# Attention on one Trainium2 core: the second exponential stays in PSUM, row sums come from rounded parts and a ones column, and groups end in fp32 products

## The chip, the cores and the metric

The kernel runs on one core of a Trainium2 chip. The metric is the time of one execution on the device in microseconds (us). The engines are TensorE (PE in the profile, with its weight loads as PEld), VectorE (DVE), ScalarE (ACT), GpSimd (POOL) and SyncE (SP), which issues transfers. Each takes its instructions in the order in which they were put down; they wait for one another by semaphores.

## What is computed

One layer of a streaming encoder, for 2048 prompt tokens and 64 sample tokens: an input projection, attention with eight heads beside a depthwise convolution, an output projection, a feed-forward block and a gated embedding. The change lies in attention. Cut to that:

```python
def attend_chunk_causal(q, k, v):            # prompt: 2048 queries, 2048 keys
    mask = k_chunk[None, :] <= q_chunk[:, None]       # chunks of 64
    sc = jnp.einsum('bqhd,bkhd->bhqk', q_blk, k).astype(jnp.float32) * scale
    pr = jax.nn.softmax(jnp.where(mask, sc, NEG), axis=-1).astype(v.dtype)
    return jnp.einsum('bhqk,bkhd->bqhd', pr, v)

def attend_open(q, k, v):                    # sample: 64 queries, 256 cached keys and 64 new ones
    sc = jnp.einsum('bqhd,bkhd->bhqk', q, k).astype(jnp.float32) * (QK_DIM ** -0.5)
    pr = jax.nn.softmax(sc, axis=-1).astype(v.dtype)
    return jnp.einsum('bhqk,bkhd->bqhd', pr, v).reshape(b, s, ATTN_W)
```

A query and a key have 96 channels, a value has 64. All is fp32.

## The kernel before

The kernel has three phases: input projection with the convolution beside it, attention (`phase2`), and the rest of the layer. To keep fp32 accuracy from a reduced product type (fp32r), a number is held as a rounded part and a rest, `hi` and `lo`; `mm3` (lines 179 to 181) makes a product as hi x hi + lo x hi + hi x lo.

Attention goes over eight heads and, in each, over five groups: four of 512 prompt queries (with 4, 8, 12 and 16 key tiles of 128) and one of the 64 sample queries (three key tiles). Per head and group there are two streams of steps. `maxima` loads the queries, makes one product of the rounded operands per 512 keys into a `tr` bank (line 714) and takes the row maxima from it on VectorE (line 715); the negated maxima go into a spare row of the queries. `attend` then goes over the key tiles. For each it makes the transposed scores (keys on partitions, up to 512 queries as columns; on the diagonal 512, 384, 256 and 128) into an `mm` bank of PSUM. ScalarE reads that bank twice: `ph` is the exponential rounded to fp32r (line 752), `px` the same exponential in fp32 (line 753), both in SBUF. VectorE makes `pl = px - ph` (line 754). GpSimd adds all `px` of the group into the first one (line 758), for the row sums. TensorE multiplies `v`, which holds the 64 hi and 64 lo columns of the values side by side, by `ph` (line 761) and by `pl` (line 762), both into the bank `acc`.

At the end of a group ScalarE copies `acc` to `ot` (line 765). TensorE transposes each token tile of `ot` (line 769), ScalarE copies one half (line 772) and VectorE adds the other (line 773). TensorE also transposes the sums (line 775), VectorE reduces them over keys to `su` (line 777) and takes reciprocals (line 779).

What sets the order: the two streams are interleaved by their columns, `maxima` running ahead by `AHEAD`; then a scheduler with a model of the chip orders the instructions of each engine. `banks` gives out the eight PSUM banks: in attention `mm` goes round two of them, then three, `tr` round four, and `acc` has one. `PXB` and `PHB` are the numbers of SBUF buffers of `px` and of `ph` and `pl`.

Of the kernel before, what the change touches and what calls it, by code (L numbers as in the profile page):

```python
# [9 lines left out]
F32 = mybir.dt.float32  # L10
# [38 lines left out]
PXB = 7  # L49
PHB = 5  # L50
# [17 lines left out]
class Body:  # L68
    def __init__(self, nc, tc, ctx, I, O):
# [10 lines left out]
        # reciprocal softmax sums of every token and head  # L80
        self.ri = self.cp.tile([P, 17, NH], F32, name="ri")

# [21 lines left out]
    def scratch(self):  # L104
# [3 lines left out]
        # scaled queries, channel-major: nope rows of all heads, then first and second halves of their rope rows  # L108
# [3 lines left out]
        # rotated keys, then the rows that meet the masks and maxima  # L112
# [4 lines left out]
    @contextmanager  # L117
    def low(self, off):
        """Instructions traced inside give way to those of the next `off`."""
        self.tc.cur_priority += off  # L120
        yield
        self.tc.cur_priority -= off

    def banks(self, mm, tr, spare):
        """PSUM banks that mm() and tr() go round, and the one of acc()."""
        self.mmi, self.tri, self.spare = cycle(mm), cycle(tr), spare
# [40 lines left out]
    def pin(self, r, n=1):  # L167
        """n steps of the background work, queued behind r on its engine."""
# [14 lines left out]
    def norms(self, xs, tiles, w=D):  # L183
        """Reciprocal root mean squares of the rows of xs (of width w), a column per tile."""
# [9 lines left out]
    def scaled(self, xs, piece, dst):  # L194
        """dst[j] = xs[j] * rstd of its rows (all of width D)."""
# [6 lines left out]
    def operand(self, piece, hs, gc, nk, hi, lo):  # L202
        """hi/lo [128, nk, N] <- transposed hs tiles times gain columns."""
# [18 lines left out]
    def phase1(self):  # L222
        nc, tc, I, O = self.nc, self.tc, self.I, self.O
        self.banks((0, 1, 2, 7), (4, 5, 6), 3)
        with ExitStack() as c:
# [13 lines left out]
            def early_t(piece, hs, i):  # L239
                """Operand of the rows as they are; their norms as columns and, along all partitions, as a row."""  # L240
# [18 lines left out]
            def weights(parts, k, c, eng=None):  # L259
                """Split weights [128, k, c]: per k, (hi, lo) [128, c]."""  # L260
# [14 lines left out]
            def rows(T, w, c, name, width):  # L275
                """Token-major products of a piece with w, to SBUF, and the sums of squares of `width` columns."""
# [20 lines left out]
            def latents(T, w):  # L297
                """c_kv of a piece; its rotated keys to scratch."""
# [20 lines left out]
            def keys(T, kvs):  # L319
                """Split transposed latents of a piece."""  # L320
# [27 lines left out]
            def queries(T, cqs):  # L348
                """Split transposed query latents of a piece; a function that makes the queries."""
# [29 lines left out]
            def glu(T, j, w, n=3):  # L379
                """Channels j of the conv input of a piece, channel-major, to scratch."""  # L380
# [24 lines left out]
            # rows of the norms of block 0, and ones  # L405
# [818 lines left out]
```

## Time and profile before

| | |
|---|---|
| three timed runs, median (lowest to highest) | 3081.51 us (3078.47 to 3082.38) |
| the profiled execution, its span | 3076.4 us |
| TensorE busy | 2940.3 us, 96% of the span |
| VectorE busy | 2047.9 us, 67% |
| ScalarE busy | 1215.2 us, 40% |
| GpSimd busy | 878.3 us, 29% |

The time of the profiled execution is its span and what lies around it. Shares of the whole span mix phases with different limits; attention goes from about 525 to 1110 us. A matmul's end is modelled, so its duration contains a fill that overlaps with the next one: TensorE's pace is read from the distances of starts. Instructions of the other engines overlap their neighbours a little as well.

### The profile page before, as it was taken

The numbers are of one execution on the slowest core, as the hardware profiler recorded it, in microseconds if no ns is written. First come the engines' busy times: TensorE is split into PE (matmuls) and PEld (weight loads), VectorE is DVE, ScalarE is ACT, GpSimd is POOL, SyncE is SP. The second block draws the span as 40 slices with busy tenths as digits, with TensorE's granted clock in tenths as the row PEclk, the third lists the DMA queues.
The fourth block names the chain that finished last, engine by engine and source line by source line (L and its number), as shares of the span: only waits on it lengthen the run. The fifth ranks groups of instructions, "written<-read, shape, count | busy, mean of one in ns | idle before, by whom it ended". The sixth has DMA issues, their size and how long they took to land.

```text
span 3076.4 us, 42553 instructions
## 1 busy us (share of the span) xinstructions
PE 2940.3 (96%) x15586; PEld 2604.4 (85%) x15586; DVE 2047.9 (67%) x3533; ACT 1215.2 (40%) x2404; POOL 878.3 (29%) x1498
## 2 busy tenths in 40 slices
PE   8998899989989879999999999999999999999998
PEld 7997888667667769999999888998998799999986
DVE  4489693999999866666665556787775544444453
ACT  6443342767666734222222433222234432321242
POOL 3235555877776730002002020003022100000001
PEclk9999999999998989999999999999999999999999
DMA  6635258743331132111222242232232411221121
GB/s 200 207 115 181 82 167 166 107 66 57 56 53 31 32 123 74 61 57 64 71 84 78 81 162 69 68 108 68 73 109 92 144 48 62 83 76 55 62 92 45
DMA packets 148601, 279.12 MB, mean 91 GB/s; under 512 B 38136, under 2 KB 78824, under 8 KB 146952
## 3 DMA queue, kind: packets, MB, share of 16 engines
q1 hardware_dynamic: 123800, 244.35, 24.7%
q0 software_dynamic: 24592, 32.06, 6.5%
q8 instruction: 122, 2.00, 0.3%
q14 instruction: 87, 0.71, 0.1%
HBM read 225.67 MB, written 51.28 MB: 90 GB/s over the span
## 4 chain that ended last, share of the span: by engine, by line
PE 72%; DVE 15%; DMA 4%; issue 4%; POOL 3%; ACT 1%; SPq 1%; DVEq 0%; POOLq 0%; ACTq 0%
PE mm L179 23%; PE mm L181 23%; PE mm L180 23%; DVE pl L754 6%; DVE mx L715 3%; DVE cacc L614 2%; PE tr L211 2%; PE tr L714 1%; PE acc L762 1%; DMA qr<-q_s 1%; DMA qr<-in_mq 1%; DMA h<-in_x 1%; POOL rt L153 0%; POOL ry L155 0%; DVE su L777 0%
## 5 line engine op out<-in xcount | busy, mean ns | idle before, releaser
L179 PE MATMUL mm<-thi,uh 128*128 128x384 f32 (+2 forms) x1488 | 480.8, 324 | 0.0
L180 PE MATMUL mm<-tlo,uh 128*128 128x384 f32 (+2 forms) x1488 | 480.7, 323 | 0.0
L181 PE MATMUL mm<-thi,ul 128*128 128x384 f32 (+2 forms) x1488 | 480.3, 323 | 0.0
L614 DVE SCALAR_TENSOR_TENSOR cacc<-cu,cw,cacc 128x384 f32<-128x384 f32 (+2 forms) x720 | 445.1, 632 | 7.3
L758 POOL TENSOR_TENSOR px<-px 128x512 f32<-128x512 f32 (+5 forms) x304 | 399.6, 1315 | 124.7 <-ACT px L753 65.4
L179 PE MATMUL mm<-wdh,ah 128*128 128x512 f32 x896 | 349.5, 391 | 4.9 <-DVE x L1060 2.9
L180 PE MATMUL mm<-wdl,ah 128*128 128x512 f32 x896 | 348.8, 390 | 0.0
L181 PE MATMUL mm<-wdh,al 128*128 128x512 f32 x896 | 345.2, 390 | 0.0
L983 ACT ACTIVATE rl<-mm 128x384 f32<-128x384 f32 (+1 forms) x192 | 88.1, 459 | 590.6 <-PE mm L181 590.2
L152 POOL TENSOR_TENSOR rt<-ry 128x3 f32<-128x3 f32 (+2 forms) x150 | 38.0, 254 | 987.0 <-DVE ry L149 980.2
L754 DVE TENSOR_TENSOR pl<-px,ph 128x512 fp32r<-128x512 f32 (+5 forms) x344 | 309.3, 913 | 15.2 <-ACT px L753 14.1
L1060 DVE SCALAR_TENSOR_TENSOR x<-mm,y,x 128x512 f32<-128x512 f32 x224 | 166.6, 749 | 206.9 <-PE mm L181 204.8
L180 PEld LDWEIGHTS mm<-tlo,uh 128*128 128x128 f32 x1488 | 280.2, 188 | 0.5
L179 PEld LDWEIGHTS mm<-thi,uh 128*128 128x128 f32 x1488 | 279.9, 188 | 0.7
L181 PEld LDWEIGHTS mm<-thi,ul 128*128 128x128 f32 x1488 | 280.1, 188 | 0.1
L165 DVE TENSOR_TENSOR wdl<-raw,wdh 128x1024 fp32r<-128x1024 f32 x139 | 170.8, 1230 | 116.7 <-ACT wdh L164 115.5
L752 ACT ACTIVATE ph<-mm 128x512 fp32r<-128x512 f32 (+5 forms) x344 | 179.3, 522 | 119.6 <-PE mm L181 102.4
L164 ACT CAST wdh<-raw 128x1024 fp32r<-128x1024 f32 x139 | 146.0, 1050 | 157.9 <-DMA raw<-in_wdn 87.1
L179 PEld LDWEIGHTS mm<-wdh,ah 128*128 128x128 f32 x896 | 168.3, 188 | 40.6 <-DVE x L1060 3.3
L181 PEld LDWEIGHTS mm<-wdh,al 128*128 128x128 f32 x896 | 168.2, 188 | 35.0
L180 PEld LDWEIGHTS mm<-wdl,ah 128*128 128x128 f32 x896 | 168.3, 188 | 33.7
L602 POOL DMA_DIRECT2D cu<-u_s x20 | 11.2, 558 | 637.9 <-DVE cacc L614 637.5
(297 smaller groups left out, 6854.4 us busy)
## 6 DMA issues: line engine op xcount, KB each, us to landing
raw<-in_wup SPq DMA_DIRECT2D x96, 512.0 KB, 3.2
raw<-in_wdn SPq DMA_DIRECT2D x96, 512.0 KB, 3.2
raw<-in_wglu SPq DMA_DIRECT2D x24, 512.0 KB, 4.6
raw<-in_wout SPq DMA_DIRECT2D x24, 512.0 KB, 4.5
raw<-in_wgate SPq DMA_DIRECT2D x24, 512.0 KB, 3.8
v_s<-vst SPq DMA_DIRECT2D x36, 256.0 KB, 2.8
v<-v_s POOLq DMA_DIRECT2D x8, 1152.0 KB, 9.2
h<-in_x SPq DMA_DIRECT2D x16, 512.0 KB, 4.5
```

The lines of the kernel that those rows point to most:

```text
L164: self.nc.scalar.copy(out=hi, in_=raw)
L165: return (eng or self.nc.vector).tensor_tensor(out=lo, in0=raw, in1=hi.bitcast(F32), op=ALU.subtract)
L179: t.matmul(ps, sh, mh, start=start, stop=False)
L180: t.matmul(ps, sh, ml, start=False, stop=False)
L181: t.matmul(ps, sl, mh, start=False, stop=stop)
L614: nc.vector.scalar_tensor_tensor(out=a, in0=U[:, k:k + W], scalar=w, in1=a, op0=ALU.mult, op1=ALU.add)
L715: nc.vector.tensor_reduce(out=mx[:n, b:b + 1] if nb > 1 else top, in_=ps[:n, :w], axis=AX.X, op=ALU.max, negate=True)
L752: nc.scalar.activation(out=ph[b:, s], in_=ps[:, s], func=AF.Exp)
L754: nc.vector.tensor_tensor(out=pl[b:, s], in0=px[b:, s], in1=ph[b:, s].bitcast(F32), op=ALU.subtract)
L758: nc.gpsimd.tensor_tensor(out=rs[b:, s], in0=rs[b:, s], in1=px[b:, s], op=ALU.add)
L983: nc.scalar.activation(out=rl[:, :N], in_=ps[:, :N], func=AF.Relu)
L1060: r = nc.vector.scalar_tensor_tensor(out=x1[t][:n, cs], in0=ps[:n, :], scalar=Y[q][:n, j:j + 1], in1=x1[t][:n, cs], op0=ALU.mult, op1=ALU.add)
```

## The change

The second exponential is written over the scores, in the same PSUM bank, in place of `px` in SBUF; `pl` reads it there. So the bank is held until `pl` is done. `v` gets two columns of ones, and its hi and lo halves change places: lo, hi, ones. The products with `ph` take all 128 value columns, as before, into `acc`; the products with `pl` take the 64 hi columns and the ones, into a bank of their own, `low`. The product of `pl` with the lo half of the values is no longer made. GpSimd adds up the `ph` in a tile `rs` of its own (a copy for the first key tile); the ones column adds up the `pl`.

A group ends in two copies by ScalarE, `ot` and `ol`, and, per token tile, three fp32 products that add up in one bank: `ol` with 65 columns of the identity, `ot` with `fold` (two identities of 64 stacked: hi plus lo), and `rs` with a column of ones. The result holds the output in 64 columns and the row sum in the 65th. ScalarE copies the output, VectorE takes the reciprocals straight from PSUM. VectorE's `o` and `su` are gone. Banks are now three for `mm`, three for `tr`, one for `acc`, one for `low`, from the start; `PHB` goes from 5 to 6 and `px` is gone.

```diff
-                nc.scalar.copy(out=v[:n, :, 0, :], in_=pv[:n, hs])
-                r = nc.vector.tensor_tensor(out=v[:n, :, 1, :], in0=pv[:n, hs], in1=v[:n, :, 0, :].bitcast(F32),
+                nc.scalar.copy(out=v[:n, :, 1, :], in_=pv[:n, hs])
+                r = nc.vector.tensor_tensor(out=v[:n, :, 0, :], in0=pv[:n, hs], in1=v[:n, :, 1, :].bitcast(F32),
...
-        self.banks((0, 1), (2, 4, 5, 6), 7)
+        self.banks((0, 1, 2), (3, 4, 5), 6)
...
-                V[i] = pool.tile([P, NKT, P], F32R, name=f"v{i}")
+                V[i] = pool.tile([P, NKT, VW], F32R, name=f"v{i}")
+                nc.vector.memset(V[i][:, :, P:].bitcast(F32), 1.0)
...
-                acc = self.acc()
+                acc, low = self.acc(), self.bank(7, "low")
+                rs = p.tile([P, 512], F32, name="rs", bufs=2)
...
-                    nc.scalar.activation(out=ph[b:, s], in_=ps[:, s], func=AF.Exp)
-                    nc.scalar.activation(out=px[b:, s], in_=ps[:, s], func=AF.Exp)
-                    nc.vector.tensor_tensor(out=pl[b:, s], in0=px[b:, s], in1=ph[b:, s].bitcast(F32), op=ALU.subtract)
+                    nc.scalar.activation(out=ph[b:, s], in_=ps[b:, s], func=AF.Exp)
+                    nc.scalar.activation(out=ps[b:, s], in_=ps[b:, s], func=AF.Exp)
+                    nc.vector.tensor_tensor(out=pl[b:, s], in0=ps[b:, s], in1=ph[b:, s].bitcast(F32), op=ALU.subtract)
                     if kt == 0:
-                        rs = px
+                        nc.gpsimd.tensor_copy(out=rs[:, s], in_=ph[:, s].bitcast(F32))
                     else:
-                        nc.gpsimd.tensor_tensor(out=rs[b:, s], in0=rs[b:, s], in1=px[b:, s], op=ALU.add)
+                        nc.gpsimd.tensor_tensor(out=rs[b:, s], in0=rs[b:, s], in1=ph[b:, s].bitcast(F32), op=ALU.add)
...
-                    nc.tensor.matmul(acc[:, s], vk, ph[b:, s], start=kt == 0, stop=False)
-                    nc.tensor.matmul(acc[:, s], vk, pl[b:, s], start=False, stop=last)
+                    nc.tensor.matmul(acc[:, s], vk[:, :P], ph[b:, s], start=first, stop=last)
+                    nc.tensor.matmul(low[:VW - 64, s], vk[:, 64:], pl[b:, s], start=first, stop=last)
...
+                ol = p.tile([P, 512], F32, name="ol", bufs=2)[:VW - 64, :]
+                nc.scalar.copy(out=ol[:, :qn], in_=low[:VW - 64, :qn])
...
-                    nc.tensor.transpose(out=tr[:n, i * P:(i + 1) * P], in_=ot[:, i * P:i * P + n], identity=self.ident)
+                    c, q = 65 * i, slice(i * P, i * P + n)
+                    nc.tensor.matmul(tr[:n, c:c + 65], ol[:, q], self.ident[:VW - 64, :65], start=True, stop=False)
+                    nc.tensor.matmul(tr[:n, c:c + 64], ot[:, q], fold, start=False, stop=False)
+                    nc.tensor.matmul(tr[:n, c + 64:c + 65], rs[:, q], one, start=False, stop=True)
...
-                nc.scalar.copy(out=o[:n, :m, :], in_=x[:, :, 1, :])
-                nc.vector.tensor_tensor(out=o[:n, :m, :], in0=x[:, :, 0, :], in1=o[:n, :m, :], op=ALU.add)
-                for i in range(m):
-                    nc.tensor.transpose(out=sm[:n, i * P:(i + 1) * P], in_=rs[:, i * P:i * P + n], identity=self.ident)
-                su = self.sp.tile([P, 4], F32, name="su")
-                nc.vector.tensor_reduce(out=su[:n, :m], in_=sm[:n, :m * P].rearrange("p (t k) -> p t k", k=P), axis=AX.X,
-                                        op=ALU.add)
-                nc.vector.reciprocal(out=self.ri[:n, tiles[0]:tiles[0] + m, h:h + 1], in_=su[:n, :m].unsqueeze(2))
+                nc.scalar.copy(out=o[:n, :m, :], in_=x[:, :, :64])
+                nc.vector.reciprocal(out=self.ri[:n, tiles[0]:tiles[0] + m, h:h + 1], in_=x[:, :, 64:])
```

The scheduler also puts the instructions in another order. TensorE before, inside the group of 16 key tiles of a head (`k0h` and `k0l` are the keys, `ph_8994` and `pl_8995` came from the scores `mm_8989`, `ph_9011` from `mm_9006`, and the scores `mm_9038` and `mm_9055` lie between these and the two shown):

```order
L179 MATMUL mm_9076<-qh_8314,k0h_5808 128x512
L180 MATMUL mm_9076<-ql_8315,k0h_5808 128x512
L181 MATMUL mm_9076<-qh_8314,k0l_5809 128x512
L714 MATMUL tr_8819<-k0h_5808,qh_8529 128x512
L714 MATMUL tr_8923<-k0h_5808,qh_8913 128x320
L179 MATMUL mm_9092<-qh_8314,k0h_5808 128x512
L180 MATMUL mm_9092<-ql_8315,k0h_5808 128x512
L181 MATMUL mm_9092<-qh_8314,k0l_5809 128x512
L762 MATMUL acc_8926<-pl_8995,v0_5812 128x512
L761 MATMUL acc_8926<-ph_9011,v0_5812 128x512
```

The product with `pl_8995` stands behind five younger score tiles. TensorE now, at the same place (`ph_8982` and `pl_8983` came from the scores `mm_8978`, `pl_8952` from `mm_8947`, `ph_8998` from `mm_8994`):

```order
L179 MATMUL mm_8994<-qh_8272,k0h_5808 128x512
L180 MATMUL mm_8994<-ql_8273,k0h_5808 128x512
L181 MATMUL mm_8994<-qh_8272,k0l_5809 128x512
L762 MATMUL acc_8868<-ph_8982,v0_5812 128x512
L763 MATMUL low_8869<-pl_8952,v0_5812 66x512
L179 MATMUL mm_9014<-qh_8272,k0h_5808 128x512
L180 MATMUL mm_9014<-ql_8273,k0h_5808 128x512
L181 MATMUL mm_9014<-qh_8272,k0l_5809 128x512
L717 MATMUL tr_8908<-k1h_5828,qh_8887 128x128
L717 MATMUL tr_8928<-k1h_5828,qh_8887 128x384
L762 MATMUL acc_8868<-ph_8998,v0_5812 128x512
L763 MATMUL low_8869<-pl_8983,v0_5812 66x512
```

A product with `ph` now follows its scores by one younger tile and one with `pl` by two; over the whole program, the products with `pl` stood behind three to seven younger tiles for most tiles, and stand behind exactly two for 292 of 344.

VectorE before, in the same stretch (`mx` are row maxima, `o` is the output of an earlier group):

```order
L754 TENSOR_TENSOR pl_8995<-px_8993,ph_8994 128x512
L754 TENSOR_TENSOR pl_9012<-px_9010,ph_9011 128x512
L773 TENSOR_TENSOR o_8734<-tr_8728,o_8734 128x256
L715 TENSOR_REDUCE mx_8752<-tr_8785 128x1
L754 TENSOR_TENSOR pl_9044<-px_9042,ph_9043 128x512
```

VectorE now:

```order
L755 TENSOR_TENSOR pl_8952<-mm_8947,ph_8951 128x512
L755 TENSOR_TENSOR pl_8983<-mm_8978,ph_8982 128x512
L718 TENSOR_REDUCE mw0_5818<-tr_8908 128x1
L718 TENSOR_REDUCE mw0_5818<-tr_8928 128x1
L755 TENSOR_TENSOR pl_8999<-mm_8994,ph_8998 128x512
```

The subtraction takes its first operand from the score bank, and the addition of `o` is gone; reductions of maxima stand between subtractions as before.

## Rows read from the trace of the kernel before

**Rows 1.** The head of the page: the span of the profiled execution.

```profile
span 3076.4 us, 42553 instructions
```

**Rows 2.** The timeline of VectorE: start us, duration us, engine, line, operation, count.

```profile
606.75 0.22 DVE L754 TENSOR_TENSOR pl<-px,ph 64x64 fp32r<-64x64 f32 x1
...
1027.12 0.22 DVE L754 TENSOR_TENSOR pl<-px,ph 64x64 fp32r<-64x64 f32 x1
```

**Rows 3.** Busy time of each engine over these six heads, granted clock, DMA.

```profile
606.75:1027.12 420.37, 382.43 (x1777) 296.52 (x1776) 395.15 (x705) 287.58 (x709) 314.82 (x246) 0.94 0.33 54
```

**Rows 4.** Waits in the same stretch: us in total, times, longest us.

```profile
PEld acc L762 <- DVE pl L754: 48.3, 81, 1.2
...
PE acc L762 <- DVE pl L754: 24.4, 52, 0.9
```

**Rows 5.** Groups by line, VectorE, same stretch: count, busy us, mean ns, idle before.

```profile
L754 DVE TENSOR_TENSOR pl<-px,ph 128x512 fp32r<-128x512 f32 (+5 forms) x258 | 230.3, 905 | 11.6 <-ACT px L753 11.4
...
L777 DVE TENSOR_REDUCE su<-tr 128x4 f32<-128x512 f32 (+1 forms) x30 | 17.5, 599 | 5.4 <-PE tr L775 5.2
...
L773 DVE TENSOR_TENSOR o<-tr,o 128x256 f32<-128x256 f32 (+1 forms) x30 | 11.0, 366 | 0.0
```

**Rows 6.** Groups by line and shape in the same stretch, GpSimd and VectorE.

```profile
L758 POOL TENSOR_TENSOR px<-px 128x512 f32<-128x512 f32 x144 | 227.1, 1577 | 73.8 <-ACT px L753 52.0 <-DVE pl L754 12.5
L754 DVE TENSOR_TENSOR pl<-px,ph 128x512 fp32r<-128x512 f32 x168 | 188.1, 1129 | 11.4 <-ACT px L753 11.4
```

**Rows 7.** Lines 773, 1110, 1111 over the whole span: ns shortest/median/longest.

```profile
L773 DVE TENSOR_TENSOR o<-tr,o x40: 183/411/425, 554.6 to 1114.0; 128x256 f32<-128x256 f32 x32, 64x64 f32<-64x64 f32 x8
...
L1110 DVE TENSOR_TENSOR rl<-mm,rl x34: 681/686/692, 1735.6 to 3063.9; 128x512 f32<-128x512 f32 x32, 64x512 f32<-64x512 f32 x2
...
L1111 DVE TENSOR_TENSOR x<-x,rl x34: 679/692/694, 1736.3 to 3064.6; 128x512 f32<-128x512 f32 x32, 64x512 f32<-64x512 f32 x2
```

**Rows 8.** The timeline of GpSimd, four additions in a row.

```profile
669.51 4.58 POOL L758 TENSOR_TENSOR px<-px 128x512 f32<-128x512 f32 x4
```

**Rows 9.** Groups by line, ScalarE, the six heads.

```profile
L753 ACT ACTIVATE px<-mm 128x512 f32<-128x512 f32 (+5 forms) x259 | 134.5, 519 | 0.8 <-POOL px L758 0.8
...
L765 ACT COPY ot<-acc 128x512 f32<-128x512 f32 (+1 forms) x31 | 17.1, 553 | 4.6 <-PE acc L762 4.4
```

**Rows 10.** The timeline of TensorE, 838 to 844 us.

```profile
838.15 0.39 PE L762 MATMUL acc<-pl,v 128*128 128x512 f32 x1
...
841.11 0.53 PE L714 MATMUL tr<-k1h,qh 128*128 128x512 f32 x2
...
843.70 0.34 PE L179 MATMUL mm<-qh,k1h 128*128 128x384 f32 x1
843.88 0.34 PE L180 MATMUL mm<-ql,k1h 128*128 128x384 f32 x1
```

**Rows 11.** The timeline of TensorE in the first phase: transposes, an fp32 product, the next.

```profile
37.09 0.82 PE L211 MATMUL tr<-ident,h 128*128 128x128 f32 x6
37.74 0.81 PE L249 MATMUL tr<-cu,cs 128*128 128x384 f32 x2
38.09 0.63 PE L179 MATMUL mm<-whi,thi 128*128 128x384 f32 x1
38.56 0.33 PE L180 MATMUL mm<-wlo,thi 128*128 128x384 f32 x1
```

**Rows 12.** Busy time in stretches (columns: PE, PEld, DVE, ACT, POOL, granted clock, DMA).

```profile
847.50:850.00 2.50, 1.90 (x9) 1.07 (x8) 2.50 (x4) 1.24 (x4) 2.42 (x2) 1.00 0.00 0
850.00:852.50 2.50, 1.71 (x7) 0.87 (x5) 2.50 (x7) 0.00 (x0) 1.91 (x3) 0.75 0.00 0
...
857.50:860.00 2.50, 2.50 (x7) 1.97 (x6) 0.69 (x1) 2.03 (x4) 0.00 (x0) 0.50 0.00 0
```

More of the change, by code (lines that the diff above doesn't have):

```diff
@@ L48 @@
 AHEAD = 16000
-PXB = 7
-PHB = 5
+PHB = 6
+VW = P + 2
 TILES = [(t * P, P) for t in range(SEQ // P)] + [(SEQ, DEC)]
@@ L675, in load_kv @@
                 v = V[h % 3]
-                nc.gpsimd.dma_start(out=v[:, :NKT - 1, :],
+                nc.gpsimd.dma_start(out=v[:, :NKT - 1, :P],
                                     in_=self.v_s[:(NKT - 1) * P, h, :].rearrange("(t p) d -> p t d", p=P))
-                nc.gpsimd.dma_start(out=v[P - DEC:, NKT - 1, :], in_=self.v_s[(NKT - 1) * P:, h, :])
+                nc.gpsimd.dma_start(out=v[P - DEC:, NKT - 1, :P], in_=self.v_s[(NKT - 1) * P:, h, :])
             def group(g):
@@ L745, in attend @@
                     self.mm3(ps[:, s], kh[:, kk], kl[:, kk], qh[:, s], ql[:, s], True, True)
-                    if kn < P:
-                        ps = ps[P - kn:, :]
-                    px = p.tile([P, 512], F32, name="px", bufs=PXB)
+                    b = P - kn
                     ph = p.tile([P, 512], F32R, name="ph", bufs=PHB)
                     pl = p.tile([P, 512], F32R, name="pl", bufs=PHB)
-                    b = P - kn
-                    nc.scalar.activation(out=ph[b:, s], in_=ps[:, s], func=AF.Exp)
-                    nc.scalar.activation(out=px[b:, s], in_=ps[:, s], func=AF.Exp)
-                    nc.vector.tensor_tensor(out=pl[b:, s], in0=px[b:, s], in1=ph[b:, s].bitcast(F32), op=ALU.subtract)
+                    nc.scalar.activation(out=ph[b:, s], in_=ps[b:, s], func=AF.Exp)
+                    nc.scalar.activation(out=ps[b:, s], in_=ps[b:, s], func=AF.Exp)
+                    nc.vector.tensor_tensor(out=pl[b:, s], in0=ps[b:, s], in1=ph[b:, s].bitcast(F32), op=ALU.subtract)
                     if kt == 0:
-                        rs = px
+                        nc.gpsimd.tensor_copy(out=rs[:, s], in_=ph[:, s].bitcast(F32))
                     else:
-                        nc.gpsimd.tensor_tensor(out=rs[b:, s], in0=rs[b:, s], in1=px[b:, s], op=ALU.add)
+                        nc.gpsimd.tensor_tensor(out=rs[b:, s], in0=rs[b:, s], in1=ph[b:, s].bitcast(F32), op=ALU.add)
                     vk = v[b:, 16 + kt if smp else kt, :]
-                    last = kt == len(kts) - 1
-                    nc.tensor.matmul(acc[:, s], vk, ph[b:, s], start=kt == 0, stop=False)
-                    nc.tensor.matmul(acc[:, s], vk, pl[b:, s], start=False, stop=last)
+                    first, last = kt == 0, kt == len(kts) - 1
+                    nc.tensor.matmul(acc[:, s], vk[:, :P], ph[b:, s], start=first, stop=last)
+                    nc.tensor.matmul(low[:VW - 64, s], vk[:, 64:], pl[b:, s], start=first, stop=last)
                     yield qn - lo * P + 60
@@ L789, in phase2 @@
                 nc.vector.memset(x.bitcast(F32), 0.0)
+            fold = p.tile([P, 64], F32, name="fold")
+            nc.vector.tensor_tensor(out=fold, in0=self.ident[:, :64], in1=self.ident[:, 64:], op=ALU.add)
+            one = p.tile([P, 1], F32, name="one")
+            nc.vector.memset(one, 1.0)
             idr = p.tile([P, P], F32R, name="idr")
@@ L821, in phase2 @@
             ca, cb = -AHEAD, 0
-            for i, c in enumerate(a):
+            for c in a:
                 ca += c
-                if i == 30:
-                    self.banks((0, 1, 2), (3, 4, 5, 6), 7)
                 while cb * wa < ca * wb:
```

4 lines of the change are left out of this document (2 added, 2 removed).

## The prediction, made before the changed kernel was run

> **What bounds the kernel now.** The span is 3076.4 us, in one execution; the three timed runs have a median of 3081.5, 5.1 more, which is what lies around the span [rows 1]. I read the attention by its stretches first, since the change touches nothing else but three small preparations. The smallest score tile of the sample's group comes back once per head: at 606.75 us and, six heads later, at 1027.12, so a head takes 420.37 / 6 = 70.06 us [rows 2]. In that stretch VectorE is busy 395.15 of 420.37 us, 94%, TensorE 382.43 (with the half-speed time in it: mean granted clock 0.94), ScalarE 287.58, GpSimd 314.82 [rows 3]. The waits agree: TensorE's weight loads and matmuls stand 48.3 and 24.4 us for `pl` of VectorE [rows 4]. VectorE sets the pace, and of its time the 258 subtractions `pl` take 230.3 us [rows 5].
>
> Why are they so dear? A 512-wide `pl` takes 1129 ns here, and GpSimd's 512-wide addition 1577 ns [rows 6]. The same VectorE operation, 512 wide with both operands in SBUF, takes 692 ns in the last phase, where GpSimd is nearly idle, and 686 ns with one operand in PSUM. And inside attention, with GpSimd as busy as ever, the one subtract-like operation that has an operand in PSUM and one in SBUF (`o`, 256 wide) stays between 183 and 425 ns over all its 40 calls, median 411 [rows 7]. GpSimd's own addition, when it runs undisturbed, takes 4.58 / 4 = 1.15 us [rows 8]. So two engines reading two SBUF operands each stretch one another, and an operand in PSUM ends that.
>
> **The change part by part**, per head, from the six-head stretch.
>
> *VectorE.* `pl` now reads the second exponential from PSUM. By the 686 ns at 512 and the 411 at 256, a column is 1.07 ns, so 384, 128 and 64 columns take .55, .27 and .21 us. The stretch has 168 tiles of 512, 24 each of 384, 256 and 128, and 18 of 64: 168 x .686 + 24 x (.55 + .41 + .27) + 18 x .21 = 149 us in place of 230. That is 81 us, 13.6 a head. The reduction `su` and the addition `o` go: 17.5 + 11.0 = 28.5, 4.8 a head [rows 5]. VectorE falls from 65.9 to 47.5 us a head, and no longer binds.
>
> *GpSimd.* 38 additions a head become up to .4 us shorter, five copies (at most 1.15 us each) come in: 50 us a head fall to about 43. Off the path.
>
> *ScalarE.* One copy `ol` of the new accumulator more per group, at the price of `ot`: 17.1 us for 31, so 5 x .55 = 2.8 a head. ScalarE goes from 47.9 to 50.7. The second exponential now writes PSUM; no row shows that. Its nearest row is the same exponential into SBUF, 519 ns; I take that, and bound it by .1 us either way, 43 tiles, 4 us a head. ScalarE would still end below TensorE [rows 9].
>
> *TensorE.* Thirteen 512-column products start from 838.15 on until the next one at 841.11: (841.11 - 838.15) / 13 = .228 us apart, those of 384 columns .18 (I use .174: 128 columns less are .054 less, so 256 take .12), and a short product is held by its weight load: six in a row take .82 us, less the .27 of the last, over 5 = .11 [rows 10, 11]. A head has, for scores and values, 5 products for each of 28 tiles of 512, and for 4 each of 384, 256 and 128, and 3 of 64: 5 x (28 x .228 + 4 x (.174 + .12 + .115) + 3 x .11) = 41.7. The maxima: 28 x .228 + 4 x (.174 + .12 + .115) and some six short ones, 8.7. The group ends: 17 tiles x 2 transposes x .12 = 4.1. Sum 54.6 of the 70.06. The change keeps the first two sums (the value products have the same columns) and replaces each pair of transposes by three fp32 products. What does such a product cost? The only fp32 product of the trace that is no transpose, 384 wide, stands as two matmuls: they start at 37.74, and the next product, which lasts .33 when nothing is ahead of it, ends at 38.72, so the pair held TensorE for .65 us [rows 11]. A pass is thus .85 ns a column: 65 columns need .055 us, less than the .11 of a weight load. So a product is two passes of .11, a token tile 6 x .11 = .66 instead of .24, and a head 17 x .42 = 7.1 us more: **61.7 us**. Beneath, if passes overlapped better, 17 x (6 x .055 - .24) = 1.5; above, if a pass cost a full .15, 11. I keep .11, the pace of the nearest row. This is the part of the change that costs.
>
> A rule speaks against this edit: the Trainium skill, "TensorE: Matmul & The Clock Gate", section Terms, says that the transpose mode is 4 times faster for fp32. By columns alone that is 4 x 130 column times for the three products against 256 for two transposes, .12 us a tile at the .445 ns of rows 10, or 2 us a head where I take 7.1; the trace shows the 4 column times in the 384-wide product, but short products are held by their weight loads.
>
> *The clock.* In each head TensorE falls to half speed (1.2 of 2.4 GHz) once: granted clock .75 and then .50 from about 851 to 861 us, after a stretch in which it waited for `pl` [rows 12]. The mean of 0.94 costs 6%, 4 us a head. With `pl` faster that stretch is denser; I count 1.5 us a head left, between 0 and 4.
>
> *The banks.* `mm` now holds a score until `pl` has read it, where a copy in SBUF freed it before. Banks for scores stay three. The order shows it: before, the product with a `pl` follows its own scores by three to seven younger tiles; now by two (292 of 344). From the last score pass, a tile needs .39 for that pass, .50 and .59 for the exponentials, .69 for `pl` and some .1 of signals, 2.3 us, and .46 for the first two passes ahead; three tiles' work on TensorE is 3 x 5 x .228 = 3.4 us without maxima, 4.1 with one each. So a slack of .7 to 1.4 us is there, and one reduction (.60) or copy ahead of the tile uses most of it. The same holds for who is queued behind: ScalarE's exponentials of the next group stand behind `ot` and `ol`, which wait for the group's last products, five times a head. I count 3 us a head of TensorE's waiting, 1.5 to 9; before it was 70.06 - 54.6 - 4 = 11.5.
>
> *At no cost:* the fill of ones, `fold` and `one` (six instructions on VectorE ahead of attention, a few us at most where it has time); the swap of the halves of `v` (same bytes, same rows of 512 bytes); the group end's wait for `rs`, which GpSimd ends within an addition (1.15) of the last exponential, while the value products with `pl` and the copy `ol` take longer. If GpSimd lagged, each of 40 group ends would stall TensorE, since products of other tiles stand behind.
>
> **The sum.** 61.7 + 1.5 + 3 = 66.2 us a head against 70.06: 3.9 x 8 heads = 31 us. 3076.4 - 31 = 3045 of span, **3050.5 us** with the 5.1. So TensorE binds after the change, and most of VectorE's gain (18 us a head) is spent: a part was slack behind TensorE, a part goes into the fp32 products.
>
> **The rivals.**
> 1. *TensorE is filled, clock full.* 61.7 + 0 + 1.5 = 63.2: -6.9 x 8 = -55, **3026**. For it: VectorE now keeps 94% busy, and TensorE would have work queued as well; cheaper fp32 products end here too. Against: three banks and in-order queues.
> 2. *The stretching stays* when the subtraction still reads one operand from SBUF, or GpSimd stretches it otherwise. Then `pl` keeps its 230 us and VectorE has 61.1 a head beside TensorE's 61.7; with 4 of clock and 4 of waits 69.7: **3078**, no change. Against: `o` in rows 7, though it is 256 wide and only 40 calls. The Trainium skill, "SBUF — State Buffer", section Who interferes with whom, says that VectorE contends with GpSimd's reads when both its inputs are in SBUF, and not when one at most is; this lowers the rival's chance, and the rows agree.
> 3. *The banks bind: slower.* If each key tile waits .2 us for its bank, 43 tiles give 8.6 a head, and the clock stays as it is (4): 61.7 + 12.6 = 74.3, +34 us, **3115**. The point from which it decides: waits and clock together above 8.4 us a head. For it: slack of .7 us beside reductions of .6. Against: VectorE and ScalarE are busy only 47.5 and 50.7 of 66.
>
> **How the numbers follow.** Forecast .50, rival 1 .20, rival 2 .12, rival 3 .18. Forecasts and rival 1 end below 3075.3, that is faster by over 0.2% (some 6 us, about what a measurement of this kernel can tell from no change): .70. Rival 2 is the .12 of the same, rival 3 the .18 of slower. The range reaches down to rival 1 less a little, 3022, and up into rival 3 to 3090, which leaves out about a tenth on each side at most.
>
> **What would show it.** In the profile after: `pl` at 512 columns near .69 us and GpSimd's addition near 1.15 (rival 2 if above .9); three fp32 products as six matmuls per token tile, .66 us; VectorE near 70% of attention and TensorE the engine that others wait for; a head near 66 us. Rival 3 shows as score products that wait for `pl` or its bank. Wrong would be a clock that drops oftener, for the short fp32 passes, or ScalarE above 60 us a head, by a dear exponential into PSUM.

## The result, and the profile after

The changed kernel takes 3049.09 us (median of four runs, 3045.0 to 3052.11) against 3081.95 for the kernel before (four runs, 3078.47 to 3085.56): a ratio of 0.9891, with a 95% interval of 0.9877 to 0.9906. The forecast was 3050.5, from 3022 to 3090, and faster. The profiled execution took 3045.0 us, with a span of 3043.2, 33.2 less than before [rows 1].

The head of the page: span, and each engine's busy time, share of the span and instructions; then the shares of the chain that ended last, by engine.

```profile
span 3043.2 us, 43503 instructions
...
PE 2960.0 (97%) x16130; PEld 2636.6 (87%) x16130; DVE 1915.9 (63%) x3458; ACT 1235.8 (41%) x2444; POOL 823.9 (27%) x1538
...
PE 83%; DVE 6%; POOL 4%; DMA 2%; ACT 2%; issue 2%; SPq 0%; ACTq 0%; POOLq 0%; DVEq 0%
```

The timeline of VectorE, with the smallest score tile of the sample's group, as in [rows 2], and under it the busy time of the engines in those six heads (PE, PEld, DVE, ACT, POOL, then granted clock, DMA share, GB/s), as in [rows 3]:

```profile
602.57 0.23 DVE L755 TENSOR_TENSOR pl<-mm,ph 64x64 fp32r<-64x64 f32 x1 [0.20 <-ACT mm L754]
...
998.70 0.23 DVE L755 TENSOR_TENSOR pl<-mm,ph 64x64 fp32r<-64x64 f32 x1 [0.74 <-ACT mm L754]
```

```profile
602.57:998.70 396.13, 392.74 (x2184) 320.49 (x2183) 301.17 (x647) 304.68 (x742) 272.56 (x278) 0.99 0.32 57
```

A head takes 396.13 / 6 = 66.02 us, 4.04 less than the 70.06 of before; eight such heads make 32.3 of the 33.2 us, so little is left for what lies outside attention. TensorE is busy 99% of the stretch, VectorE 76% (94% before).

Groups of instructions in the six heads (count, busy us, mean ns of one, idle before it and what ended that): by line the subtractions; by line and shape, of 512 columns, GpSimd's additions and the subtractions; by line two of ScalarE:

```profile
L755 DVE TENSOR_TENSOR pl<-mm,ph 128x512 fp32r<-128x512 f32 (+5 forms) x259 | 147.0, 575 | 42.8 <-ACT mm L754 40.5
```

```profile
L759 POOL TENSOR_TENSOR rs<-rs,ph 128x512 f32<-128x512 f32 x144 | 185.5, 1288 | 73.2 <-ACT ph L753 66.7
...
L755 DVE TENSOR_TENSOR pl<-mm,ph 128x512 fp32r<-128x512 f32 x168 | 113.9, 683 | 28.5 <-ACT mm L754 26.8
```

```profile
L754 ACT ACTIVATE mm<-mm 128x512 f32<-128x512 f32 (+5 forms) x258 | 131.5, 510 | 0.4
...
L769 ACT COPY ol<-low 66x512 f32<-66x512 f32 (+1 forms) x30 | 15.3, 509 | 0.0
```

The subtraction at 512 columns fell from 1129 to 683 ns and its group from 230.3 to 147.0 us [rows 5, 6]. It now waits 40.5 us for the second exponential, where it waited 11.4 before [rows 5]. TensorE's weight loads stood 48.3 us for `pl` before [rows 4]; these are waits of its weight loads after:

```profile
PEld acc L762 <- ACT ph L753: 9.1, 25, 0.7
PEld mm L179 <- DVE pl L755: 2.5, 3, 1.1
...
PEld low L763 <- DVE pl L755: 1.4, 5, 0.3
```

The last row is the wait that was 48.3 us. The second is the score bank: a score product that waits for the subtraction to free it. It happened three times in six heads. The first, the longest in total, is of products with `ph`, which wait for ScalarE's first exponential.

The timeline of TensorE in a group end, two token tiles:

```profile
777.05 0.44 PE L774 MATMUL tr<-ident,ol 66*128 66x65 f32 x2
777.32 0.39 PE L775 MATMUL tr<-fold,ot 128*128 128x64 f32 x2
777.55 0.33 PE L776 MATMUL tr<-one,rs 128*128 128x1 f32 x2
777.74 0.41 PE L774 MATMUL tr<-ident,ol 66*128 66x65 f32 x2
```

A token tile's products come .67 to .69 us apart, and every product is two matmuls, whether it has 65 columns or one.

### The profile page after: what moved, and what is told of

Its sections match the earlier page's. It is cut to its first block, busy times and chain, and to the rows that moved or that the text cites. A ratio compares the mean times of both kernels' runs of the same rounds, so it can differ in the third digit from the quotient of the medians.

```text
span 3043.2 us, 43503 instructions
## 1 busy us (share of the span) xinstructions
PE 2960.0 (97%) x16130; PEld 2636.6 (87%) x16130; DVE 1915.9 (63%) x3458; ACT 1235.8 (41%) x2444; POOL 823.9 (27%) x1538
## 4 chain that ended last, share of the span: by engine, by line
PE 83%; DVE 6%; POOL 4%; DMA 2%; ACT 2%; issue 2%; SPq 0%; ACTq 0%; POOLq 0%; DVEq 0%
PE mm L179 24%; PE mm L181 24%; PE mm L180 24%; DVE cacc L614 3%; PE acc L762 2%; PE tr L717 2%; PE low L763 2%; PE tr L211 2%; PE tr L774 1%; PE tr L775 1%; ACT ph L753 1%; PE tr L776 1%; POOL rt L153 1%; POOL ry L155 1%; POOL rt L154 0%
## 5 line engine op out<-in xcount | busy, mean ns | idle before, releaser
L759 POOL TENSOR_TENSOR rs<-rs,ph 128x512 f32<-128x512 f32 (+5 forms) x304 | 324.8, 1071 | 106.8 <-ACT ph L753 89.7
L755 DVE TENSOR_TENSOR pl<-mm,ph 128x512 fp32r<-128x512 f32 (+5 forms) x344 | 195.4, 577 | 66.4 <-ACT mm L754 63.7
L718 DVE TENSOR_REDUCE mx<-tr 128x1 f32<-128x512 f32 (+3 forms) x288 | 170.2, 615 | 41.5 <-PE tr L717 40.9
```

The source lines that it names most:

```text
L718: nc.vector.tensor_reduce(out=mx[:n, b:b + 1] if nb > 1 else top, in_=ps[:n, :w], axis=AX.X, op=ALU.max, negate=True)
L755: nc.vector.tensor_tensor(out=pl[b:, s], in0=ps[b:, s], in1=ph[b:, s].bitcast(F32), op=ALU.subtract)
L759: nc.gpsimd.tensor_tensor(out=rs[b:, s], in0=rs[b:, s], in1=ph[b:, s].bitcast(F32), op=ALU.add)
```

## The experiments

"Head" below is a sixth of the stretch between the same small tiles of six heads. "Clock lost" is worked out from the windows of such a stretch, 2.5 us each: the sum of (1 - granted clock) x time. It was 23.9 us in the six heads before, 4.0 a head, and 5.1 after, .85 a head. "Waits" is what is left of a head beside TensorE's own sum (61.7 in the changed kernel, by the forecast) and the clock: 70.06 - 54.6 - 4.0 = 11.5 before, 66.02 - 61.7 - .85 = 3.5 after. So an error in the 61.7 would show as waits. All ratios are to the kernel before, run on the same chip, with the 95% interval in brackets. Differences from the changed kernel go by its 3049.09 us; since the kernel before came to between 3078 and 3082 us from one set of runs to the next, a difference of some 4 us there says little. Figures of a head come from one profiled execution of each kernel.

### Is it the operand in PSUM? The kernel before without the additions

```diff
                     if kt == 0:
                         rs = px
-                    else:
-                        nc.gpsimd.tensor_tensor(out=rs[b:, s], in0=rs[b:, s], in1=px[b:, s], op=ALU.add)
```

> The kernel before without GpSimd's additions: the row sums hold the first key tile's exponentials alone, and one is added to them in place of the reciprocal, so the output is another. Theory: pl, still with two SBUF operands, falls from 1.13 to .69 us at 512 columns because GpSimd reads nothing beside it; VectorE 52 us a head, TensorE 54.6 and some 4 of waits and clock, head 58 to 60 us, 2985 to 3003 us. Rival (the place of the operand alone makes pl slow, whatever GpSimd does): pl stays at 1.13 us and the time at 3082 us.

It took 2980.92 us, 0.9682 [0.9667, 0.9696], a little below the theory's range: a head is 56.82 us, 2.2 above TensorE's 54.6, and no clock is lost in it. The group of the subtractions, both operands still in SBUF, by shape:

```profile
L754 DVE TENSOR_TENSOR pl<-px,ph 128x512 fp32r<-128x512 f32 x168 | 113.4, 682 | 20.5 <-ACT px L753 20.1
```

682 ns, the same as with an operand in PSUM (683). So 447 of the 1129 ns were GpSimd's doing, and the additions as a whole cost the kernel before 97 us, three times what the change brings.

### The changed kernel with the second exponential in SBUF

```diff
-                    nc.scalar.activation(out=ps[b:, s], in_=ps[b:, s], func=AF.Exp)
-                    nc.vector.tensor_tensor(out=pl[b:, s], in0=ps[b:, s], ...
+                    px = p.tile([P, 512], F32, name="px", bufs=PXB)
+                    nc.scalar.activation(out=px[b:, s], in_=ps[b:, s], func=AF.Exp)
+                    nc.vector.tensor_tensor(out=pl[b:, s], in0=px[b:, s], ...
```

> The changed kernel with one thing put back: the second exponential goes to SBUF again (px, four buffers; to make room ph and pl have five buffers and ol one) and pl reads two SBUF operands. Theory (two SBUF operands beside GpSimd's reads stretch both engines): pl of 512 columns at 1.1 us instead of .68, GpSimd's addition at 1.5, VectorE near 61 us a head beside TensorE's 62, so a head of 69 to 70 us instead of 66.0 and 3073 to 3081 us. Rival (the gain comes from the operations taken from VectorE at group ends and from the new order of banks): a head stays at 66 us, 3049 us, or gets shorter, since the bank is free earlier.

It took 3114.53 us, 1.0127 [1.0108, 1.0146]: the theory's side, but 35 us above its numbers. Its six heads, its additions and subtractions by shape, and the subtractions by line:

```profile
618.32:1051.30 432.98, 410.01 (x2180) 324.52 (x2179) 397.00 (x643) 296.21 (x739) 323.56 (x279) 0.97 0.32 52
```

```profile
L761 POOL TENSOR_TENSOR rs<-rs,ph 128x512 f32<-128x512 f32 x144 | 223.3, 1551 | 30.3 <-ACT ph L754 21.8
L757 DVE TENSOR_TENSOR pl<-px,ph 128x512 fp32r<-128x512 f32 x168 | 198.8, 1198 | 4.6 <-ACT px L756 4.5
```

```profile
L757 DVE TENSOR_TENSOR pl<-px,ph 128x512 fp32r<-128x512 f32 (+5 forms) x258 | 251.2, 992 | 6.1 <-ACT px L756 4.5 <-ACT o L781 1.1
```

The stretching is back: 1198 and 1551 ns. VectorE is busy 66.2 us of a head of 72.2, where the theory had 61.1: the subtractions take 251.2 us, not the 230.3 of before [rows 5] that it took over, which is 3.5 of the 5.1. The clock lost 2.3 us a head and the waits are 8.2. How much of these is due to fewer buffers (four of `px`, where the kernel before has seven, five of `ph` and `pl`, one of `ol`) was not separated. What can be said is that with these buffers the rest of the change, without the operand in PSUM, is slower than the kernel before; and that the operand, with the buffers it saves, is worth 65 us.

### What do the fp32 products cost? Group ends by transposes

Three transposes a token tile (`ot`, `ol`, `rs`), and VectorE adds the parts and reduces the sums:

```diff
-                    nc.tensor.matmul(tr[:n, c:c + 65], ol[:, q], self.ident[:VW - 64, :65], start=True, stop=False)
-                    nc.tensor.matmul(tr[:n, c:c + 64], ot[:, q], fold, start=False, stop=False)
-                    nc.tensor.matmul(tr[:n, c + 64:c + 65], rs[:, q], one, start=False, stop=True)
+                    nc.tensor.transpose(out=tr[:n, i * P:(i + 1) * P], in_=ot[:, i * P:i * P + n], identity=self.ident)
+                    nc.tensor.transpose(out=tl[:n, i * 66:(i + 1) * 66], in_=ol[:, i * P:i * P + n], identity=self.ident[:66, :66])
+                    nc.tensor.transpose(out=sm[:n, i * P:(i + 1) * P], in_=rs[:, i * P:i * P + n], identity=self.ident)
+                nc.vector.tensor_tensor(out=o[:n, :m, :], in0=y[:, :, :64], in1=o[:n, :m, :], op=ALU.add)
...
```

> The changed kernel with the six fp32 passes per token tile at the group's end replaced by three transposes (of ot, ol and rs), and VectorE adding the two halves and the ol part, reducing the sums over keys, and adding the ones column. Theory (TensorE binds, a pass or transpose costs .11 to .12 us): 17 x (.67 - .36) = 5.3 us a head less on TensorE, VectorE rises from 50 to about 57 a head and stays below; head 60.7 us, about 3007 us. Rival (a group end now takes all three tr banks, so the maxima wait, or VectorE's queue becomes late): head 64 to 66 us, 3033 to 3049 us.

It took 3020.28 us, 0.981 [0.9794, 0.9827], and is the same computation. It beats both kernels. Its six heads:

```profile
607.43:982.21 374.78, 361.12 (x1873) 283.95 (x1872) 326.06 (x763) 305.25 (x738) 272.60 (x278) 0.98 0.37 60
```

A head is 62.46, 3.56 less, between the theory's 60.7 and the rival's 64. By an estimate of .36 us for three transposes (three times the forecast's .12), TensorE's sum falls by 17 x (.66 - .36) = 5.1 to 56.6; 1.1 of the head is lost clock and 4.7 are waits, 1.2 more than in the changed kernel. Among these, products for the maxima wait 7.4 us in six heads for ScalarE's `qh`, against .5 in the changed kernel. VectorE pays 4.1 a head (54.3 for 50.2) and stays below TensorE. The fp32 products saved VectorE time it had and cost TensorE time it had not.

### One fp32 product more, and the same time in long products

The first fp32 product of each token tile twice:

```diff
+                    nc.tensor.matmul(tr[:n, c:c + 65], ol[:, q], self.ident[:VW - 64, :65], start=True, stop=True)
                     nc.tensor.matmul(tr[:n, c:c + 65], ol[:, q], self.ident[:VW - 64, :65], start=True, stop=False)
```

> The changed kernel with the first fp32 product of each token tile at a group's end made twice (the first result is overwritten). Theory (TensorE binds, each fp32 product costs two passes of .11 us): 17 x .22 = 3.8 us a head more, head 69.8 us, 3079 us. Rival (TensorE has waits to take it up, or VectorE and ScalarE bind): 3049 to 3055 us.

It took 3107.17 us (3098.22 to 3116.24), 1.0093 [1.0068, 1.0119]: 58 us more than the changed kernel, where the theory had 30. A head is 73.36, 7.3 more. The timeline of TensorE behind a group end that ran without a gap from 636.10 on, and the windows there:

```profile
639.39 0.33 PE L777 MATMUL tr<-one,rs 128*128 128x1 f32 x2
639.59 0.30 PE L725 MATMUL tr<-idr,mw 128*128 128x128 f32 x1
639.73 0.36 PE L717 MATMUL tr<-k1h,qh 128*128 128x320 f32 x1
639.93 0.70 PE L763 MATMUL low<-pl,v 128*66 128x512 f32 x2
640.43 0.63 PE L762 MATMUL acc<-ph,v 128*128 128x512 f32 x1
640.85 0.63 PE L763 MATMUL low<-pl,v 128*66 128x512 f32 x1
```

```profile
636.42:638.92 2.50, 2.50 (x25) 2.50 (x24) 1.47 (x4) 1.23 (x3) 2.35 (x2) 1.00 0.16 42
638.92:641.42 2.50, 2.50 (x15) 2.02 (x15) 0.57 (x2) 1.40 (x5) 0.19 (x1) 0.79 0.06 13
641.42:643.92 2.50, 2.50 (x8) 1.83 (x7) 0.00 (x0) 0.21 (x1) 0.00 (x0) 0.53 0.18 39
```

The 512-column products that follow stand .43 apart instead of .23, at a granted clock of .53, so near the 1.2 GHz level; and TensorE had been busy all the while. The clock lost 4.0 us a head here, against .85: 3.1 of the 7.3. Waits are 3.9, near the 3.5 of the changed kernel. In the changed kernel itself the same drop is to be seen, three times in six heads, each time behind a group end during which TensorE was busy throughout. One of the three:

```profile
672.57:675.07 2.50, 2.50 (x11) 1.68 (x11) 1.67 (x3) 2.49 (x7) 2.28 (x3) 0.53 1.01 177
```

Is it TensorE's added time as such, or the short products? The next kernel adds the same time in long one-pass products behind each token tile:

```diff
                     nc.tensor.matmul(tr[:n, c + 64:c + 65], rs[:, q], one, start=False, stop=True)
+                    for _ in range(2):
+                        nc.tensor.matmul(tr[:n, 260:], idr[:, :n], kh[:, :252], start=True, stop=True)
```

> The changed kernel with two more one-pass products behind each token tile's three at a group end, 252 columns wide (.12 us each by the 256 of the forecast), whose results are not read: .24 us a token tile, as much of TensorE's time as the doubled fp32 product took (two passes of .11). That one cost 58 us where its passes sum to 30, and the granted clock fell in almost every head. Theory (it falls behind short passes, which wait for their weight loads): long products add their own time alone, 17 x .24 x 8 = 33 us, 3076 to 3085 us, clock lost no more than the .85 us a head of the changed kernel. Rival (any more time of TensorE at a group end costs double, by banks and queues): 3100 to 3112.

It took 3078.07 us (ten runs, 3071.46 to 3086.36), 0.9991 [0.9979, 1.0002]: 29 us more than the changed kernel, as expected of the theory. A head is 69.81, 3.79 more. The starts of two token tiles on TensorE, and its six heads:

```profile
775.62 0.33 PE L774 MATMUL tr<-ident,ol 66*128 66x65 f32 x2
...
776.20 0.48 PE L778 MATMUL tr<-k0h,idr 128*128 128x252 f32 x2
776.52 0.33 PE L774 MATMUL tr<-ident,ol 66*128 66x65 f32 x2
```

```profile
611.92:1030.76 418.84, 410.70 (x2388) 340.86 (x2387) 299.91 (x646) 305.81 (x742) 272.82 (x279) 1.00 0.26 54
```

The granted clock is full in every window: with long products among the short ones even the .85 us is gone. Over the whole span the mean granted clock was .974 to .979 in the four runs with one fp32 product more, and .984 to .991 in these ten. A group end of four token tiles holds TensorE about as long in both: 3.5 us there (636.10 to 639.59), 4 x .90 = 3.6 here. A token tile takes .90 us instead of .67, and 17 x .23 = 3.9 us is what a head is longer by. So time of TensorE at a group end is paid in full, and in these two kernels the short fp32 passes cost clock on top. What in the short passes lets the clock fall stays open, and the scheduler may order the two kernels differently; shown is that the kernel with them loses clock, and the one with long passes of the same time does not.

### Do the score banks bind? Two, three and four

```diff
-        self.banks((0, 1, 2), (3, 4, 5), 6)
+        self.banks((0, 1), (2, 3, 4, 5), 6)
```

> The changed kernel with two banks for scores instead of three (and four instead of three for the row maxima and group ends). A score bank is now held from its first pass to the end of the subtraction: .85 us of passes, .50 and .51 of exponentials, .68 of subtraction and some .2 of signals, 2.7 us for a full tile. Theory (the banks are near their limit): two banks give at best a tile per 1.37 us, what TensorE needs with one maxima product each (1.14 + .23), so every delay now stalls TensorE: 2 to 8 us a head more, 3065 to 3113 us. Rival (the waits left in the changed kernel, some 3.5 us a head, come from the group ends and not from the banks, and two would do): 3043 to 3055.

3164.72 us, 1.0274 [1.0258, 1.0289]. A head is 81.46, of which 5.4 is lost clock and 14.4 are waits. The waits of TensorE's weight loads in its six heads:

```profile
PEld acc L762 <- ACT ph L753: 43.0, 80, 1.0
PEld low L763 <- DVE pl L755: 21.7, 53, 1.0
```

In 80 and 53 of 258 tiles a value product waits for its exponential or its subtraction, while the score products hardly wait for a bank (1.1 us in 6 waits). My reading, which no run separates, is that with two tiles in flight the scheduler has less of other tiles to put ahead of a value product. The theory was right in its sign and too low in its size: 81.46 is more than the price of the forecast's third rival (74.3 us a head), which had looked for the wait at the score products. One of its terms was short: a full tile's exponentials take .60 us each in the changed kernel, and .50 and .51 are means over all widths.

```diff
-        self.banks((0, 1, 2), (3, 4, 5), 6)
+        self.banks((0, 1, 2, 3), (4, 5), 6)
```

> The changed kernel with four banks for scores, and only two for the row maxima and group ends. Theory (half or more of the 3.5 us a head that TensorE still waits comes from score banks): 2 to 3 us a head less, 3025 to 3035 us. Rival 1 (the waits come from the group ends, where TensorE waits for the copies of the accumulators): 3043 to 3055. Rival 2 (two banks for the maxima bind, since a reduction holds one for .68 us and VectorE's queue is in order): slower, 3065 to 3100.

3186.68 us, 1.034 [1.0325, 1.0356]. A head is 83.6 (three heads from 610.96 to 861.75), of which 14.2 is lost clock. The largest wait of its weight loads in the three heads:

```profile
PEld tr L717 <- DVE mx L718: 19.2, 31, 1.3
```

Two banks for the maxima bind, as the second rival of that run said, at a higher price than it gave: products of maxima wait for reductions, and the mean granted clock of these heads is 0.83. Whether a fourth score bank by itself would gain remains open, since all eight banks are given out.

### Spreading the group ends

The forecast put a part of the waits at the group end, where ScalarE's exponentials stand behind the copies of the accumulators. Here one token tile's six passes go behind each of the next group's first key tiles, into a bank of their own, which leaves two for the maxima:

```diff
+                    if pend:
+                        pend.pop(0)()
                     yield qn - lo * P + 60
...
-                tr = self.tr()
+                tr = self.bank(5, "te")
```

> The changed kernel with the same fp32 products, but not all four token tiles of a group end at once: one token tile's six passes behind each of the first key tiles of the next group, into a bank of their own (two are left for the row maxima). For the last head they stay together. Theory (the clock falls behind the cluster of short products, and TensorE waits at a group end for the copies of the accumulators): the .85 us a head of clock goes, and 1 of the 3.5 us of waits: 64.2 instead of 66.0 us a head in seven heads, 3049 - 13 = 3036 us (3030 to 3042). Rival 1 (the clock falls by the number of short products, wherever they stand): 3045 to 3055. Rival 2 (two banks for the maxima bind): slower than 3060; the kernel with four score banks shows that by itself.

3106.53 us, 1.0072 [1.0052, 1.0092]. Two banks for the maxima are in it as well, so by itself it tells nothing; its counterpart has the same banks, and the ends together:

> The changed kernel with the group ends together as they are, but in a bank of their own, which leaves two for the row maxima: the kernel with spread ends (3106.5 us), not spread. Theory (two banks for the maxima bind, and spreading itself does little): 3095 to 3120 us. Rival (the spreading costs it, as short products between the long ones slow these): 3045 to 3065 us.

3089.46 us, 1.0037 [1.0024, 1.005], a little below the theory's range. A bank less for the maxima costs some 40 us; spreading costs another 17. A head is 73.95 spread and 72.35 together. The six heads of both, the spread one first:

```profile
611.25:1054.93 443.68, 425.81 (x2183) 349.95 (x2181) 299.49 (x642) 308.44 (x739) 270.39 (x277) 0.90 0.32 51
```

```profile
609.39:1043.47 434.08, 417.10 (x2180) 342.15 (x2179) 299.33 (x643) 308.75 (x739) 271.09 (x277) 0.92 0.30 51
```

The clock lost is 7.4 and 6.0 us a head, the waits 4.9 and 4.7. My idea that spreading helps fell: spread, the short passes cost more clock, and the waits did not get fewer. It is no clean test of the cluster as the cause, since behind the short tiles of the sample's group the pieces still stand close together: three token tiles' products start between 612.01 and 614.63, and the clock falls at 614.26, with TensorE busy throughout.

### Two tries at the transposed version

Its sums by products with the ones column in place of transposes and a reduction:

```diff
-                    nc.tensor.transpose(out=sm[:n, i * P:(i + 1) * P], in_=rs[:, i * P:i * P + n], identity=self.ident)
+                    nc.tensor.matmul(tl[:n, 300 + i:301 + i], rs[:, i * P:i * P + n], one, start=True, stop=True)
```

> The second experiment's kernel (groups end by transposes), but the row sums of the rounded parts by fp32 products with the ones column, 17 a head, instead of transposes and a reduction on VectorE; a group end then uses two banks instead of three. Theory (what is left is TensorE's own sum): a product is two passes of .11 and a transpose one of .12, so 17 x .10 = 1.7 us a head more, 3020 + 14 = 3034 us (3028 to 3038). Rival (VectorE's five reductions of .6 us a head and the third bank hold TensorE up): up to 3 us a head less, 3000 to 3015.

3034.96 us, 0.9846 [0.9831, 0.9861]: the theory's number, but not by its reason. A head is 62.78, only .32 above 62.46 (TensorE 1.7 more, clock .85 less, waits .5 less), 2.6 us in eight. At the small tile of the last head it is only .59 us behind (1053.44 against 1052.85), while its span is 14.1 longer: nearly all of the difference comes after that tile. The first 100 us from there, of this kernel and then of the transposed one:

```profile
1053.44:1153.44 100.00, 91.63 (x432) 75.47 (x433) 44.48 (x85) 36.67 (x64) 11.84 (x53) 0.91 0.29 100
```

```profile
1052.85:1152.85 100.00, 96.19 (x480) 81.03 (x479) 50.82 (x88) 42.27 (x72) 12.27 (x51) 1.00 0.36 121
```

There 9 us of clock are lost, and TensorE is idle 4.6 us longer. Why the end of attention and the passage to the next phase came out worse stays open.

The other adds the parts first, so that two transposes a token tile are left:

```diff
-                nc.scalar.copy(out=ot[:, :qn], in_=acc[:, :qn])
+                nc.scalar.copy(out=ot[64:, :qn], in_=acc[64:, :qn])
+                nc.vector.tensor_tensor(out=ot[:64, :qn], in0=acc[:64, :qn], in1=ol[:64, :qn], op=ALU.add)
+                nc.gpsimd.tensor_tensor(out=rs[64:65, :qn], in0=rs[64:65, :qn], in1=ol[64:65, :qn], op=ALU.add)
...
```

> Groups that end by transposes, but the parts are added before: VectorE adds the small accumulator to the lower half of the large one (64 x 512, .69 us) while copying it, GpSimd adds its row of sums to one row of the partial sums, and then two transposes a token tile are left, as in the kernel before, in two banks. Against the kernel with three transposes TensorE has 17 x .12 = 2.0 us a head less, VectorE .9 more (.69 for .41 and .1, five times). Theory (TensorE's own sum is what is left): 62.5 - 2.0 = 60.5 us a head, 3020 - 16 = 3004 us (3000 to 3010). Rival (the longer chain of copies and additions ahead of the transposes takes it back): 3015 to 3035.

3019.91 us, 0.9811 [0.9795, 0.9828], the same as with three transposes, as the rival had it. A head of the profiled execution, at 3028.13 us the slowest of the four, is 61.86 where 60.5 was expected; the waits rose from 4.7 to 6.7. Weight loads of TensorE in its six heads:

```profile
PEld low L763 <- DVE pl L755: 8.3, 21, 1.2
PEld mm L179 <- DVE pl L755: 7.8, 14, 1.0
```

TensorE now waits for the subtractions, and for the score banks they hold: 7.8 us in 14 waits, against .6 in 2 with three transposes. VectorE, with the addition of the parts in its queue, is busy 335.45 of the 371.15 us, 90%. Whether the waits come from that, or from TensorE having less of its own to do, was not separated.

## Why the prediction was right

- **VectorE bound, and an operand in PSUM frees it: right, and shown** from both sides, by the kernel without additions (682 ns) and by the exponential put back into SBUF (1198). The group was put at 149 us and took 147.0. The Trainium skill, "SBUF — State Buffer", section Who interferes with whom, has a VectorE instruction with two inputs in SBUF contend with a GpSimd instruction that reads SBUF, and one with at most one such input, outside its two-port modes, not. The traces agree, with 1198 against 683 ns. VectorE's total came to 50.2 us a head, not 47.5: the groups overlap where one instruction follows another, so its busy time fell by 94 us where the groups lost 107.
- **GpSimd:** its addition was to come near 1.15 us and came to 1.29, from 1.58 [rows 6]. The 1.15 was a misreading of [rows 8]: the four additions there are not all 512 columns wide, and VectorE's subtractions ran beside them. By line and shape, GpSimd's additions from 669.52 to 674 us of the kernel before; and under them one of its 512-column additions at a time when VectorE did nothing (1073.84 to 1076.74):

```profile
L758 POOL TENSOR_TENSOR px<-px 128x512 f32<-128x512 f32 x1 | 1.6, 1618 | 0.1
L758 POOL TENSOR_TENSOR px<-px 128x384 f32<-128x384 f32 x1 | 1.3, 1342 | 0.1
L758 POOL TENSOR_TENSOR px<-px 128x256 f32<-128x256 f32 x1 | 0.9, 927 | 0.1
L758 POOL TENSOR_TENSOR px<-px 128x128 f32<-128x128 f32 x1 | 0.5, 458 | 0.1
```

```profile
1075.28 1.28 POOL L758 TENSOR_TENSOR px<-px 128x512 f32<-128x512 f32 x1
```

  So 1.28 to 1.29 us is what such an addition takes undisturbed, and with the operand in PSUM the stretching is gone on this engine too. Its additions and copies together take 43.3 us a head, against 43 forecast, but by luck: the additions are longer than forecast, and a copy takes .59 us on the mean where up to 1.15 had been taken. It is off the path.
- **ScalarE:** 50.8 us a head against 50.7. The exponential into PSUM took 510 ns, where 519 had been taken and 419 to 619 left open.
- **TensorE, 61.7 a head: right as far as it was measured.** The whole sum was not measured by itself. The term that rested on the thinnest row, .66 us a token tile from two passes of .11, came out at .67. By the Trainium skill, "TensorE: Matmul & The Clock Gate", section Terms, transposing would be 4 times faster for fp32. By columns alone that gave 2 us a head, where the forecast took 7.1; .67 against the .24 of two transposes is 17 x .43 = 7.3. A product of 65 columns holds TensorE .25 to .27 us and one of a single column still .19: short products are paid mostly by the pass.
- **The clock,** 1.5 us a head, lay at .85. But the reason was only half of it. Before, the clock fell where TensorE had waited [rows 12], and these falls did go. After, it fell behind group ends where TensorE had not waited. The forecast named that danger only in its last sentence; one product more would have brought it (4.0 us a head).
- **The waits,** 3 us a head from 1.5 to 9, lay at 3.5, which is a remainder and not a measurement. The reason given holds in part. The score banks are near their limit, since two cost 15 us a head more; but with three the bank itself stopped TensorE only three times in six heads, .4 us a head. More of the waits, 1.5 us a head, are value products that wait for the first exponential; that ScalarE's queue would do this the forecast said of the group ends, and how many of the 25 waits stand there was not separated.
- **The sum,** 66.2 a head and 3045 of span, came to 66.02 and 3043.2; errors of .65 in the clock and .5 in the waits go against each other, so that the sum is closer than its terms: that much is luck.
- The forecast's remark that most of VectorE's gain would be spent in the fp32 products was right as well, and is the change's weak spot: with transposes it brings 58 us where it brought 33.

## What to carry to other kernels

Where VectorE and GpSimd both work from SBUF, look at one operation of each beside its undisturbed time, and move one operand into PSUM before moving work; then ask which engine is next, and don't give it the work that was saved. Short fp32 products are paid by the pass more than by the column, and a transpose plus additions on an engine with time to spare can be cheaper. Banks have to suffice for both loops that share them: one taken from either cost more here than the whole change gave.

## What was not expected of the hardware

TensorE's clock fell to near its lower level behind stretches of short fp32 products with no wait in them: .53 granted after the group end at 636.10 to 639.59, and 4.0 us lost a head. With two 252-column products behind each token tile, in place of the repeated short one, none was lost: useless work kept the clock up, though it did not give the time back. And the loss is no smooth price of the waits: the spread version waits 4.9 us a head and loses 7.4 of clock, the version with parts added first waits 6.7 and loses .6.
